# Layer 0's x and the later x 64 bytes apart in one array, a head's diagonal and first level in one matmul, and another order of layer 0

## The chip, the core and the metric

The kernel runs on one core of a Trainium2 chip, in one launch. The metric is the device time of that launch in microseconds (us). Before the change it is 2133.09 us, the median of three runs (2132.8 to 2133.53).

## What is computed

A decoder trunk of two layers in float32 for 256 tokens of 2048 features. Layer 0 has two kinds of mixer side by side, fed by one projection. The change touches the second kind, the HGRN2 heads (8 heads, 128 wide), and the order in which both kinds are worked off. Cut to these:

```python
def recurrent_mixers(h, w_in, ...):
    proj = h @ w_in
    x_lru, y_lru, q_h, f_h, v_h, g_h = jnp.split(proj, list(IN_SPLITS), axis=-1)
    lru = rg_lru(causal_depthwise_conv(x_lru, conv_w, conv_b), w_a, b_a, w_i, b_i, lam)
    lru = lru * jax.nn.gelu(y_lru, approximate=True)
    hg = hgrn2(q_h, f_h, v_h, g_h, lower_bound, g_norm)
    return jnp.concatenate([lru, hg], axis=-1) @ w_out

def hgrn2(q_raw, f_raw, v_raw, g_raw, lower_bound, g_norm):
    q = jax.nn.silu(q_raw)
    log_f = jnp.log(lower_bound + (1.0 - lower_bound) * jax.nn.sigmoid(f_raw))
    k = (1.0 - lower_bound) * jax.nn.sigmoid(-f_raw)
    ...  # scores[t, s] = sum over features of q[t] k[s] f[s+1]...f[t], for s <= t
    o = scores @ v
    o = o * rsqrt(mean(o * o) + NORM_EPS) * g_norm
    return o * jax.nn.silu(g_raw)
```

After the mixers come the output projection, a squared-ReLU MLP, a second layer with dilated attention and another MLP, and a last norm.

## The kernel before

**Matmuls.** The weights arrive as float32 in units of 128 x 2048. Each unit is split into a high part (`hi`, a cast on ScalarE, L112) and the rest (`lo`, a subtraction on VectorE, L113). The activations are split in the same way, and three matmuls, all by L196, stand for one product. x of layer 0 lies in `bufa`, 16 blocks of 2 x 256 columns. Later the same array holds the inputs of layer 0's MLP, of the attention and of layer 1's MLP. Where the output is wanted by features (`project`, L346), x is the moving operand with 256 columns; where it is wanted by tokens (`tokens_group`, L339), the weights move with 512.

**Layer 0.** `ORDER` (L1077) lists the steps: `v` and `k` are four units each for the values and gates of four heads, `h` is a head (two units, q and f), `x` and `y` are an LRU block's input and output (one unit each), `g` is the two LRU gates of four blocks, with one unit of small weights and `bufb` as the moving operand. The same list orders the weights' loads on SP's queue, two units ahead of their use. The order of single instructions on each engine is then made by a scheduler, which puts the matmuls of one head between those of the following projections.

**A head** (`hgrn`, L436). With q, k and f over the features (128 partitions) and 256 tokens, the scores are built by doubling. `pd` (L454) is the product of k and q of which the diagonal is kept (L456). Then for c = 1, 2, 4, ... 128 two matmuls of 64 columns (L470, and L465 with 128 columns for the last) give the scores between neighbouring blocks of c tokens. They are put into `st` under a mask (L473) or by copies (L478, L480), q and k are multiplied by the products of f over a block (L487), and those products are doubled (L489). Before level 1 q is multiplied by f (L458). At the end `po` multiplies the scores with the values (L494 to L496), and the result is normed and turned by TensorE (L508) into `bufb`. A matmul of f32 operands shows as two records of TensorE, each with a weight load; the projections' show as one.

Of the kernel before, what the change touches and what calls it, by code (L numbers as in the profile page):

```python
# [10 lines left out]
F32 = mybir.dt.float32  # L11
F32R = mybir.dt.float32r
# [4 lines left out]
OP = mybir.AluOpType  # L17
# [3 lines left out]
P = 128  # L21
S = 256
D = 2048
KB = D // P
# [18 lines left out]
def trunk_kernel(ctx, tc, begin, xtok, cols, tab, masks, pos, fin, w_in, w_gate, w_out, w_qkv, w_o, w1, w2, out):  # L43
# [3 lines left out]
    act = pool("act")  # L47
# [11 lines left out]

    xall = act.tile([P, KB * S], F32, name="xall")  # L60
    xres = xall.rearrange("p (j d) -> p j d", j=2)
    bufa = act.tile([P, KB, 2 * S], F32R, name="bufa")

    units = []
    made = {}
# [102 lines left out]
    def fetch_first():  # L168
        r = opening.tile([P, 14, WIDE], F32, name="first")
        e = wraw.tile([P, 2048], F32, name="raw")[:, :2 * WIDE].rearrange("p (k s) -> p k s", s=WIDE)  # L170
        homes = [r[:, k] for k in range(14)] + [e[:, k] for k in range(2)]
        nc.sync.dma_start(r[:, 0, :S], begin[:, 0, :S])
        nc.sync.dma_start(r[:, 0, S:], begin[:, 0, S:])
        for k in range(1, 4):
            nc.sync.dma_start(r[:, k], begin[:, k])
        for k in range(4, 16, 2):
            nc.sync.dma_start(r[:, k:k + 2] if k < 14 else e, begin[:, k:k + 2])
        for u in range(4):
            at[0] += 1
            w = made[u] = Weights(None, 0)  # L180
            for k in range(4 * u, 4 * u + 4):
                split_to(bufa[:, k], homes[k][:, :S], col("nmix0", k))
                w.split((k - 4 * u) * 512, 512, homes[k][:, S:])

    def unit(src, i):
# [52 lines left out]
    def split_to(dst, src, gain=None):  # L238
        if gain is None:
            h, l = dst[..., :S], dst[..., S:]  # L240
            A.copy(h, src)
            V.tensor_tensor(l, src, h.bitcast(F32), OP.subtract)
        else:
            A.activation(dst[:, :S], src, AF.Copy, scale=gain)
            V.scalar_tensor_tensor(dst[:, S:], src, gain, dst[:, :S].bitcast(F32),  # L245
                                   op0=OP.mult, op1=OP.subtract)
# [89 lines left out]
        return ps  # L336

    def tokens_group(src, i0, rt=None, by_k=False, name="vg"):
        ps = tokens(src, i0, bufa, by_k)  # L339
        v = vgs.tile([P, 2, 512], F32, name=name)  # L340
        with urgent():
            for j in range(2):
                A.activation(v[:, j], ps[j], AF.Copy, scale=1.0 if rt is None else rt[:, j:j + 1])
        return v

    def project(src, i, mov):  # L346
        w = unit(src, i)
        p = pmm.tile([P, 512], F32, name="p")
        direct(p, w, [(k, mov[:, k], k == 0, k == KB - 1) for k in range(KB)])
        return p  # L350
# [85 lines left out]
    def hgrn(hd, vg, gg):  # L436
        u0 = 20 + (hd // 4) * 16 + (hd % 4) * 2
        oml = omlb[:, hd:hd + 1]
        qk = wk.tile([P, 2 * S], F32, name="qk", bufs=3)
        qp, kq = qk[:, :S], qk[:, S:]  # L440
        p = project(w_in, u0, bufa)
        z = normed(p, "hz", 4)
        lut(qp, z, AF.Sigmoid)
        V.scalar_tensor_tensor(qp, z, oml, qp, op0=OP.mult, op1=OP.mult)
        p = project(w_in, u0 + 1, bufa)
        z = normed(p, "hz", 4)
        f = wk.tile([P, S], F32, name="f", bufs=3)
        lut(f, z, AF.Sigmoid)
        lut(kq, z, AF.Sigmoid, scale=-1.0)
        V.tensor_scalar(f, f, oml, lb[:, hd:hd + 1], op0=OP.mult, op1=OP.add)  # L450
        pd = psc.tile([P, 2, P], F32, name="pd", bufs=1)
        for j in range(2):
            js = slice(j * P, j * P + P)
            T.matmul(pd[:, j], kq[:, js], qp[:, js], start=True, stop=True)  # L454
        st = wk.tile([P, 3, P], F32, name="st", bufs=3)
        V.tensor_tensor(st[:, :2], pd, ident[:, None, :].to_broadcast([P, 2, P]), OP.mult)  # L456
        stf = st[:, :2].rearrange("p a b -> p (a b)")
        V.tensor_tensor(qp, qp, f, OP.mult)  # L458
        c = 1
        tot = f  # L460
        while c <= 128:
            pl = psc.tile([P, 2, 64], F32, name="pl", bufs=2)
            if c == 128:
                plf = pl.rearrange("p j c -> p (j c)")
                T.matmul(plf, kq[:, :P], qp[:, P:], start=True, stop=True)  # L465
                A.copy(st[:, 2], plf)
                break
            for j in range(2):
                js = slice(j * P, j * P + P)
                T.matmul(pl[:, j], kq[:, js], halves(qp[:, js], c, True), start=True, stop=True)  # L470
            if c <= 16:
                lv = LEVELS.index(c)
                V.copy_predicated(halves(stf, c, True), msk[:, lv].rearrange("p (n c) -> p n c", c=c),  # L473
                                  pl.rearrange("p j (n c) -> p (j n) c", c=c))
            elif c == 32:
                for n in range(2):
                    ps_ = slice(64 * n, 64 * n + 32)
                    A.copy(st[ps_, :2, 64 * n + 32:64 * n + 64], pl[ps_, :, 32 * n:32 * n + 32])  # L478
            else:
                A.copy(st[:64, :2, 64:], pl[:64])  # L480
            n = S // (2 * c)
            tt = tot.rearrange("p (n two) -> p n two", two=2)
            both = bass.AP(tensor=qk.tensor, offset=qk.offset + c,
                           ap=[list(qk.ap[0]), [S - c, 2], [2 * c, n], [1, c]])
            fac = bass.AP(tensor=tot.tensor, offset=tot.offset,
                          ap=[list(tot.ap[0]), [1, 2], [2, n], [0, c]])
            V.tensor_tensor(both, both, fac, OP.mult)  # L487
            nt = wk.tile([P, n], F32, name=f"tot{n}", bufs=2)
            V.tensor_tensor(nt, tt[:, :, 0], tt[:, :, 1], OP.mult)  # L489
            tot = nt  # L490
            c *= 2
        vs = slice((hd % 4) * P, (hd % 4) * P + P)
        po = psc.tile([P, 2, P], F32, name="po", bufs=1)
        T.matmul(po[:, 0], st[:, 0], vg[:, 0, vs], start=True, stop=True)  # L494
        T.matmul(po[:, 1], st[:, 2], vg[:, 0, vs], start=True, stop=False)  # L495
        T.matmul(po[:, 1], st[:, 1], vg[:, 1, vs], start=False, stop=True)  # L496
        o = wk.tile([P, 2, P], F32, name="ho", bufs=2)
        hs = wk.tile([P, 2], F32, name="hs", bufs=2)
        for j in range(2):
            A.activation(o[:, j], po[:, j], AF.Square, accum_out=hs[:, j:j + 1])  # L500
        V.tensor_scalar(hs, hs, 1.0 / P, EPS, op0=OP.mult, op1=OP.add)
        hr = wk.tile([P, 2], F32, name="hr", bufs=2)
        rsqrt(hr, hs, 2)
        for j in range(2):
            V.scalar_tensor_tensor(o[:, j], po[:, j], hr[:, j:j + 1], gg[:, j, vs], op0=OP.mult, op1=OP.mult)
        pt = psc.tile([P, 2, P], F32, name="pt", bufs=1)
        for j in range(2):
            T.transpose(pt[:, j], o[:, j], ident)  # L508
        split_to(bufb[:, 8 + hd], pt.rearrange("p j c -> p (j c)"), col("gn", hd))
# [1 line left out]
    xc = wk.tile([P, 8, S], F32, name="xc", bufs=1)  # L511

    def lru_in(b):
        p = project(w_in, b, bufa)
        xp = wk.tile([P, S + 4], F32, name="xp", bufs=1)
        V.memset(xp[:, :4], 0.0)
        scaled(p, xp[:, 4:])
        A.activation(xc[:, b], xp[:, 4:], AF.Identity, bias=col("conv_b", b), scale=col("conv_w", 24 + b))
        for i in range(3):
            V.scalar_tensor_tensor(xc[:, b], xp[:, 1 + i:1 + i + S], col("conv_w", 8 * i + b), xc[:, b],  # L520
                                   op0=OP.mult, op1=OP.add)
        split_to(bufb[:, b], xc[:, b])
# [24 lines left out]
            V.tensor_tensor_scan(xc[:, b], gr[:, m], xc[:, b], 0.0, op0=OP.mult, op1=OP.add)  # L547

    def lru_out(b):
        p = project(w_in, 8 + b, bufa)  # L550
        y = tmp.tile([P, S], F32, name="z")
        scaled(p, y)
        q = wk.tile([P, S], F32, name="q", bufs=1)
        A.activation(q, y, AF.Square, scale=math.sqrt(0.044715))
        V.scalar_tensor_tensor(q, q, 1.0, y, op0=OP.add, op1=OP.mult)
        lut(q, q, AF.Sigmoid, scale=2.0 * math.sqrt(2.0 / math.pi))
        V.tensor_tensor(y, y, q, OP.mult)
        V.tensor_tensor(y, y, xc[:, b], OP.mult)
        split_to(bufb[:, b], y)
# [509 lines left out]

LAST = 2  # L1070
EARLY = 12
BOUNDARY = 56
PRIO = 150
URGENT = 400
ATTENTION = "qqvqqv"
ORDER = "v0 k0 h0 h1 h2 x1 x3 h3 x0 k1 v1 x2 h4 x4 g0 x5 h5 h6 x6 y0 y1 h7 x7 g1 y3 y7 y4 y2 y5 y6"
WARM = 12  # L1077
WAIT_H, WAIT_X, WAIT_Q, WAIT_S = 5, 2, 5, 3
SCRATCH = 4096
# [109 lines left out]
```

## Time and profile before

| | us |
|---|---|
| median of three runs | 2133.09 |
| the profiled execution | 2133.06 |
| its span, first to last instruction | 2131.3 |
| TensorE busy in it | 2120.9 |
| VectorE busy | 1788.8 |
| ScalarE busy | 1378.2 |

Layer 0's mixers take about the first 332 us; the output projection begins there. A row of the timeline has a start in us from the start of the span, a length from the first start to the last end of its instructions, the engine, the line, what is written and read, the shape and a count. TensorE's instructions overlap, so two rows are compared by their starts. PEld is TensorE's weight load.

### The profile page before, as it was taken

Reading aid. Unit: us, or ns where it says so; the run is one execution under the profiler, and the core shown is the slowest. Engines: PE = TensorE matmul, PEld = TensorE weight load, DVE = VectorE, ACT = ScalarE, POOL = GpSimd, SP = SyncE. Lnnn points to the kernel's source line nnn. Section 1 sums busy time; section 2 is a strip of 40 time slices with the busy share of each in tenths; the row PEclk is TensorE's granted clock in tenths of the full one; section 3 lists DMA queues with packets and bytes.
Section 4 is the critical chain, followed back from the end, with each engine's and each line's share of the span. In section 5 each row is a group of like instructions: output and inputs, shape, how many; then the busy total and the mean of one; then the engine's idle time right before and its main releaser. Section 6 shows DMA issues by size and latency. Waiting matters only on the chain.

```text
span 2131.3 us, 26730 instructions
## 1 busy us (share of the span) xinstructions
PE 2120.9 (100%) x10542; PEld 1797.6 (84%) x10542; DVE 1788.8 (84%) x1962; ACT 1378.2 (65%) x1543; POOL 66.8 (3%) x85
## 2 busy tenths in 40 slices
PE   9999999999999999999999999999999999999998
PEld 8989998888888888888888888888888888888886
DVE  7777888888888888888988797788897888888887
ACT  7445565776476567567666777776756765755764
POOL 0000000000000000000000000000000000000000
PEclk9999999999999999999999999999999999999999
DMA  8444446686777677677887767777767768777773
GB/s 336 162 162 158 161 148 224 206 269 233 227 237 253 230 240 253 227 241 231 270 279 218 241 199 247 254 247 228 246 237 253 236 212 269 238 234 227 271 225 146
DMA packets 69806, 488.71 MB, mean 229 GB/s; under 512 B 7808, under 2 KB 8320, under 8 KB 11952
## 3 DMA queue, kind: packets, MB, share of 16 engines
q1 hardware_dynamic: 58176, 410.96, 51.1%
q0 software_dynamic: 11216, 75.70, 18.3%
q8 instruction: 82, 1.34, 0.3%
q14 instruction: 44, 0.36, 0.0%
q10 hardware_dynamic: 288, 0.34, 0.0%
HBM read 482.78 MB, written 4.19 MB: 228 GB/s over the span
## 4 chain that ended last, share of the span: by engine, by line
PE 99%; DVE 0%; ACT 0%; DMA 0%; issue 0%; ACTq 0%; DVEq 0%; POOLq 0%
PE p L196 62%; PE po L196 14%; PE pd L196 13%; PE pt L196 5%; PE pl L199 2%; PE pl L470 1%; PE pl L196 0%; PE pd L199 0%; DMA ppi<-in_pos 0%; PE pd L454 0%; DVE lo L113 0%; ACT hi L112 0%; PE pl L465 0%; PE po L495 0%; PE po L496 0%
## 5 line engine op out<-in xcount | busy, mean ns | idle before, releaser
L113 DVE TENSOR_TENSOR lo<-raw,hi 128x2048 fp32r<-128x2048 f32 (+2 forms) x397 | 787.1, 1991 | 164.5 <-ACT hi L112 159.4
L112 ACT CAST hi<-raw 128x2048 fp32r<-128x2048 f32 (+2 forms) x397 | 657.3, 1671 | 335.1 <-PE p L196 175.5
L196 PE MATMUL p<-hi,bufa 128*128 128x512 f32 x1488 | 482.0, 394 | 0.0
L196 PE MATMUL p<-hi,bufb 128*128 128x512 f32 x1128 | 363.1, 391 | 0.0
L196 PEld LDWEIGHTS p<-hi,bufa 128*128 128x128 f32 x1488 | 279.2, 188 | 57.3 <-DVE bufa L245 0.5
L113 DVE TENSOR_TENSOR lo<-s,hi 128x2048 fp32r<-128x2048 f32 (+1 forms) x164 | 285.9, 1753 | 28.6 <-ACT hi L112 27.6
L112 ACT CAST hi<-s 128x2048 fp32r<-128x2048 f32 (+1 forms) x164 | 242.7, 1480 | 98.2 <-DVE s L164 54.2
L196 PE MATMUL p<-lo,bufa 128*128 128x512 f32 x744 | 287.6, 390 | 0.2 <-DVE lo L113 0.2
L196 PEld LDWEIGHTS p<-hi,bufb 128*128 128x128 f32 x1128 | 211.7, 188 | 43.7
L196 PE MATMUL p<-lo,bufb 128*128 128x512 f32 x564 | 219.5, 389 | 0.0
L196 PE MATMUL p<-bufa,hi 128*128 128x256 f32 x1024 | 193.2, 287 | 0.0
L196 PEld LDWEIGHTS p<-lo,bufa 128*128 128x128 f32 x744 | 139.9, 188 | 28.0 <-DVE lo L113 0.7
L196 PEld LDWEIGHTS p<-bufa,hi 128*128 128x128 f32 x1024 | 161.2, 191 | 0.2
L196 PE MATMUL p<-bufa,lo 128*128 128x256 f32 x512 | 146.5, 286 | 0.0
L112 ACT CAST hi<-t 128x2048 fp32r<-128x2048 f32 x41 | 78.5, 1914 | 99.6 <-PE p L196 91.1
L113 DVE TENSOR_TENSOR lo<-t,hi 128x2048 fp32r<-128x2048 f32 x41 | 94.0, 2292 | 55.4 <-ACT hi L112 55.0
L196 PEld LDWEIGHTS p<-lo,bufb 128*128 128x128 f32 x564 | 105.9, 188 | 21.5
L196 PE MATMUL p<-hi,formh 128*128 128x512 f32 x368 | 120.7, 391 | 0.0
L196 PE MATMUL p<-hi,formx 128*128 128x512 f32 x352 | 115.9, 390 | 0.0
L196 PE MATMUL po<-hi,bufb 128*128 128x512 f32 x320 | 103.7, 390 | 0.0
L196 PEld LDWEIGHTS p<-bufa,lo 128*128 128x128 f32 x512 | 98.0, 191 | 0.0
L164 DVE TENSOR_TENSOR s<-s,raw 128x1024 f32<-128x1024 f32 x82 | 96.4, 1216 | 0.1
(319 smaller groups left out, 3292.4 us busy)
## 6 DMA issues: line engine op xcount, KB each, us to landing
raw<-in_w SPq DMA_DIRECT2D x224, 1024.0 KB, 6.1
raw<-in_w_in SPq DMA_DIRECT2D x44, 1024.0 KB, 4.8
raw<-in_w_qkv SPq DMA_DIRECT2D x42, 1024.0 KB, 6.9
t<-in_w SPq DMA_DIRECT2D x32, 1024.0 KB, 4.9
t<-in_w POOLq DMA_DIRECT2D x32, 1024.0 KB, 8.7
s<-in_w POOLq DMA_DIRECT2D x17, 1024.0 KB, 8.4
raw<-in_w_out SPq DMA_DIRECT2D x15, 1024.0 KB, 4.8
raw<-in_w_o SPq DMA_DIRECT2D x14, 1024.0 KB, 7.7
```

The source lines that it names most:

```text
L112: a = A.copy(h, w)
L113: v = V.tensor_tensor(l, w, h.bitcast(F32), OP.subtract)
L164: V.tensor_tensor(s, s, held["c"][:, at:at + 1024], OP.add)
L196: chain[:] = [after(T.matmul(*args, **kw), chain)]
L199: chain[:] = [after(T.transpose(out_, in_, ident), chain)]
L470: T.matmul(pl[:, j], kq[:, js], halves(qp[:, js], c, True), start=True, stop=True)
```

## The change

Three edits. First, the array for x is 16 floats (64 bytes) longer. Layer 0 reads and writes it from its start (`bufx`), everything later 64 bytes further on (`bufa`). What is allocated behind it moves by 64 bytes. Second, a head keeps q in groups of three: the two tokens of a pair, and the second one multiplied by its f. One matmul of 192 columns for each half of the tokens then gives the diagonal and level 1 together, and the loop of levels starts at c = 2. Third, `ORDER` is another one.

```diff
-    bufa = act.tile([P, KB, 2 * S], F32R, name="bufa")
+    bufa_ = act.tile([P, KB * 2 * S + APART], F32R, name="bufa")
+    bufx, bufa = (bufa_[:, o:o + KB * 2 * S].rearrange("p (k c) -> p k c", k=KB) for o in (0, APART))
...
-        V.scalar_tensor_tensor(qp, z, oml, qp, op0=OP.mult, op1=OP.mult)
-        p = project(w_in, u0 + 1, bufa)
+        q3 = wk.tile([P, P, 3], F32, name="q3", bufs=2)
+        pairs_ = lambda t: t.rearrange("p (n two) -> p n two", two=2)
+        V.scalar_tensor_tensor(q3[:, :, :2], pairs_(z), oml, pairs_(qp), op0=OP.mult, op1=OP.mult)
+        p = project(w_in, u0 + 1, bufx)
...
-        pd = psc.tile([P, 2, P], F32, name="pd", bufs=1)
+        f2 = pairs_(f)
+        V.tensor_tensor(q3[:, :, 2], q3[:, :, 1], f2[:, :, 1], OP.mult)
+        pd = psc.tile([P, P, 3], F32, name="pd", bufs=1)
         for j in range(2):
-            js = slice(j * P, j * P + P)
-            T.matmul(pd[:, j], kq[:, js], qp[:, js], start=True, stop=True)
+            js = slice(64 * j, 64 * j + 64)
+            T.matmul(pd[:, js].rearrange("p n c -> p (n c)"), kq[:, j * P:j * P + P],
+                     q3[:, js].rearrange("p n c -> p (n c)"), start=True, stop=True)
         st = wk.tile([P, 3, P], F32, name="st", bufs=3)
-        V.tensor_tensor(st[:, :2], pd, ident[:, None, :].to_broadcast([P, 2, P]), OP.mult)
+        V.tensor_tensor(st[:, :2].rearrange("p j (n two) -> p j n two", two=2),
+                        pd[:, :, :2].rearrange("p (j n) c -> p j n c", j=2),
+                        pairs_(ident)[:, None].to_broadcast([P, 2, 64, 2]), OP.mult)
         stf = st[:, :2].rearrange("p a b -> p (a b)")
-        V.tensor_tensor(qp, qp, f, OP.mult)
-        c = 1
-        tot = f
+        V.copy_predicated(halves(stf, 1, True), msk[:, 0].rearrange("p (n c) -> p n c", c=1), pd[:, :, 2:])
+        V.tensor_tensor(pairs_(qp), q3[:, :, ::2], f2[:, :, :1].to_broadcast([P, P, 2]), OP.mult)
+        V.tensor_tensor(pairs_(kq)[:, :, 0], pairs_(kq)[:, :, 0], f2[:, :, 1], OP.mult)
+        tot = wk.tile([P, P], F32, name="tot128", bufs=2)
+        V.tensor_tensor(tot, f2[:, :, 0], f2[:, :, 1], OP.mult)
+        c = 2
...
+APART = 16
...
-ORDER = "v0 k0 h0 h1 h2 x1 x3 h3 x0 k1 v1 x2 h4 x4 g0 x5 h5 h6 x6 y0 y1 h7 x7 g1 y3 y7 y4 y2 y5 y6"
+ORDER = "v0 k0 h0 h1 h2 x1 x3 x2 h3 x0 v1 k1 h4 h5 h6 x4 g0 x5 x6 y0 h7 y1 x7 y2 g1 y7 y4 y3 y5 y6"
```

The other changed lines put `bufx` for `bufa` in layer 0's projections. In the new program lines are numbered a little higher (L196 becomes L197, L470 becomes L481, L494 to L496 become L505 to L507). The lists below are parts of the instruction order of the two built programs; x2 is a count. From the output projection on, TensorE's list is the same in both.

TensorE at the second head's diagonal, before (`pd` the diagonal, `pl` a level, `p` a projection):

```order
L196 MATMUL p<-bufa,lo 128x256
L196 MATMUL p<-bufa,hi 128x256
L454 MATMUL pd<-qk 128x128
L470 MATMUL pl<-qk 128x64 x2
L454 MATMUL pd<-qk 128x128
L196 MATMUL p<-bufa,hi 128x256
```

The same place now:

```order
L197 MATMUL p<-bufa,lo 128x256
L197 MATMUL p<-bufa,hi 128x256
L481 MATMUL pl<-qk 128x64 x2
L459 MATMUL pd<-q_825,qk 128x192 x2
L197 MATMUL p<-bufa,hi 128x256
```

The diagonal's two matmuls have 192 columns, and a head has six levels of two 64-column matmuls where it had seven.

TensorE at group 1 of the LRU gates (moving operand `bufb`), before. `po` is the end of head 6, the `pl` of 128x128 its last level, and the `pl` of 128x64 levels of head 7:

```order
L196 MATMUL p<-bufb,hi 128x256 x2
L196 MATMUL p<-bufb,lo 128x256
L494 MATMUL po<-vg,st 128x128
L465 MATMUL pl<-qk 128x128
L470 MATMUL pl<-qk 128x64 x2
L495 MATMUL po<-vg,st 128x128
L496 MATMUL po<-vg,st 128x128
L196 MATMUL p<-bufb,hi 128x256
L470 MATMUL pl<-qk 128x64 x2
L196 MATMUL p<-bufb,hi 128x256
```

The first rows of group 1 now. Between this pair of level matmuls and the next there are 15 gate matmuls, then 24 to the one after:

```order
L197 MATMUL p<-bufb,hi 128x256 x2
L197 MATMUL p<-bufb,lo 128x256
L481 MATMUL pl<-qk 128x64 x2
L197 MATMUL p<-bufb,hi 128x256 x2
L197 MATMUL p<-bufb,lo 128x256
```

Only levels of head 7 stand between the gates of group 1 now; the last level and the end of a head have moved out of them.

TensorE at group 0 of the gates, before (the end of head 3 and a level of head 4):

```order
L196 MATMUL p<-bufb,lo 128x256
L465 MATMUL pl<-qk 128x128
L494 MATMUL po<-vg,st 128x128
L470 MATMUL pl<-qk 128x64 x2
L196 MATMUL p<-bufb,hi 128x256 x2
```

And now (`pd` is the diagonal of head 6, `po` and the `pl` of 128x128 the end of head 5):

```order
L197 MATMUL p<-bufb,hi 128x256 x2
L459 MATMUL pd<-q_2421,qk 128x192 x2
L197 MATMUL p<-bufb,lo 128x256
L197 MATMUL p<-bufb,hi 128x256 x2
L197 MATMUL p<-bufb,lo 128x256
L197 MATMUL p<-bufb,hi 128x256
L505 MATMUL po<-vg,st 128x128
L197 MATMUL p<-bufb,hi 128x256
L476 MATMUL pl<-qk 128x128
L481 MATMUL pl<-qk 128x64 x2
```

A head's diagonal has come in among the gates of group 0, close to the end of another head.

More of the change, by code (lines that the diff above doesn't have):

```diff
@@ L181, in fetch_first @@
             for k in range(4 * u, 4 * u + 4):
-                split_to(bufa[:, k], homes[k][:, :S], col("nmix0", k))
+                split_to(bufx[:, k], homes[k][:, :S], col("nmix0", k))
                 w.split((k - 4 * u) * 512, 512, homes[k][:, S:])
@@ L338, in tokens_group @@
     def tokens_group(src, i0, rt=None, by_k=False, name="vg"):
-        ps = tokens(src, i0, bufa, by_k)
+        ps = tokens(src, i0, bufx, by_k)
         v = vgs.tile([P, 2, 512], F32, name=name)
@@ L440, in hgrn @@
         qp, kq = qk[:, :S], qk[:, S:]
-        p = project(w_in, u0, bufa)
+        p = project(w_in, u0, bufx)
         z = normed(p, "hz", 4)
         lut(qp, z, AF.Sigmoid)
-        V.scalar_tensor_tensor(qp, z, oml, qp, op0=OP.mult, op1=OP.mult)
-        p = project(w_in, u0 + 1, bufa)
+        q3 = wk.tile([P, P, 3], F32, name="q3", bufs=2)
+        pairs_ = lambda t: t.rearrange("p (n two) -> p n two", two=2)
+        V.scalar_tensor_tensor(q3[:, :, :2], pairs_(z), oml, pairs_(qp), op0=OP.mult, op1=OP.mult)
+        p = project(w_in, u0 + 1, bufx)
         z = normed(p, "hz", 4)
@@ L513, in lru_in @@
     def lru_in(b):
-        p = project(w_in, b, bufa)
+        p = project(w_in, b, bufx)
         xp = wk.tile([P, S + 4], F32, name="xp", bufs=1)
@@ L549, in lru_out @@
     def lru_out(b):
-        p = project(w_in, 8 + b, bufa)
+        p = project(w_in, 8 + b, bufx)
         y = tmp.tile([P, S], F32, name="z")
```

## The prediction

> **What bounds the kernel now.** I read the page's busy times first, then its chain of work, then a table of stages (the windows view: busy time and instruction count of each engine in a stretch).
>
> ```profile
> PE 2120.9 (100%) x10542; PEld 1797.6 (84%) x10542; DVE 1788.8 (84%) x1962; ACT 1378.2 (65%) x1543; POOL 66.8 (3%) x85
> PE 99%; DVE 0%; ACT 0%; DMA 0%; issue 0%; ACTq 0%; DVEq 0%; POOLq 0%
> 51.40:100.00 48.60, 48.60 (x410) 48.60 (x409) 34.89 (x72) 21.45 (x33) 0.00 (x0) 1.00 0.48 172
> 200.00:250.00 50.00, 50.00 (x426) 50.00 (x425) 44.98 (x124) 34.07 (x65) 0.00 (x0) 1.00 0.43 149
> 282.00:289.00 7.00, 6.74 (x52) 6.05 (x51) 6.41 (x16) 5.64 (x16) 0.00 (x0) 1.00 0.42 149
> 332.00:2131.00 1799.00, 1790.43 (x8155) 1485.14 (x8153) 1531.90 (x1321) 1188.13 (x1198) 65.89 (x80) 1.00 0.73 237
> ```
>
> TensorE is busy all the time and is 99% of the chain, at the full clock. VectorE comes next, with free time in every stage (45 of 50 us at most). A time is won here only if TensorE issues less, or if a wait between its matmuls goes. Nothing behind about 332 us can change by the edits: in the lists of the built programs TensorE's rows from the output projection to the end are the same ones in the same order, so those 1799 us stay. What follows is about the first 332 us, the mixers of layer 0.
>
> TensorE's busy time hides small waits, because the ends of pipelined matmuls are modelled. I therefore count from start to start. First the prices of one matmul. From the chain in order of time (start, us, what), two runs of 512 columns, the first with bufa's tiles and the second with bufb's:
>
> ```profile
> 447.79 5.44 PE pd L196 x24
> 552.07 13.60 PE p L196 x60
> ```
>
> TensorE's timeline (start, us from first start to last end, count) around a level of a head and around a diagonal; each x2 that "..." leaves out is two hi of 256 columns:
>
> ```profile
> 71.15 0.28 PE L196 MATMUL p<-bufa,lo 128*128 128x256 f32 x1
> ...
> 71.51 0.28 PE L196 MATMUL p<-bufa,lo 128*128 128x256 f32 x1
> ...
> 71.87 0.55 PE L470 MATMUL pl<-qk 128*128 128x64 f32 x4
> 72.23 0.36 PE L196 MATMUL p<-bufa,lo 128*128 128x256 f32 x1
> ...
> 72.68 0.28 PE L196 MATMUL p<-bufa,lo 128*128 128x256 f32 x1
> ...
> 67.83 0.28 PE L196 MATMUL p<-bufa,lo 128*128 128x256 f32 x1
> 67.95 0.28 PE L196 MATMUL p<-bufa,hi 128*128 128x256 f32 x1
> 68.07 0.61 PE L454 MATMUL pd<-qk 128*128 128x128 f32 x4
> 68.43 0.36 PE L196 MATMUL p<-bufa,hi 128*128 128x256 f32 x1
> 68.63 0.28 PE L196 MATMUL p<-bufa,lo 128*128 128x256 f32 x1
> ```
>
> 512 columns take 13.60 / 60 = 0.227 us, and 5.44 / 24 as well. 256 columns take 0.12 (71.15 to 71.51 is one lo and two hi). One f32 matmul of a head shows as two records, so x4 is two matmuls. From the lo at 71.15 to that at 72.68 are 1.53 us, of which nine matmuls of 256 columns are 1.08, so four records of 64 columns cost 0.45. From 67.83 to 68.63 are 0.80 us, three of them 256-column ones (0.36), so four records of 128 columns cost 0.44. Both are **0.11 us a record**: below 128 columns a head's matmul costs the same whatever its width.
>
> **Part 1: one matmul of 192 columns in place of 128 and 64.** Each of 8 heads loses four records of level 1 (0.44) and has its diagonal's four records widened from 128 to 192. No row has 192. The nearest on the wide side are the attention scores of layer 1, where x4 is two records of 128 and two of 256:
>
> ```profile
> 1154.29 0.39 PE L196 MATMUL p<-lo,bufa 128*128 128x512 f32 x1
> 1154.51 0.39 PE L196 MATMUL p<-hi,bufa 128*128 128x512 f32 x1
> 1154.74 0.81 PE L196 MATMUL pl<-kT,qT 128*128 128x128 f32 x4
> 1155.21 0.58 PE L196 MATMUL pt<-hi,formx 128*128 128x512 f32 x1
> 1155.62 0.39 PE L196 MATMUL pt<-lo,formx 128*128 128x512 f32 x1
> ```
>
> 1155.62 - 1154.29 = 1.33 us, less three matmuls of 512 columns (0.68), less two records of 128 (0.22), leaves 0.43 or 0.215 a record of 256. So 192 lies between 0.11 and 0.215. I take the middle, 0.163, since 128 and 256 are equally near. A head then pays 4 x 0.163 = 0.65 where it paid 0.44 + 0.44 = 0.88: 0.23 less, **1.8 us in eight heads**. With 0.11 it would be 3.5, with 0.215 only 0.2.
>
> [...]
>
> **VectorE in a head.** The rows of before for what is replaced (durations least/median/most, in ns):
>
> ```profile
> L487 DVE TENSOR_TENSOR qk<-qk,tot x48: 396/418/474, 77.9 to 312.6; 128x256 f32<-128x256 f32 x48
> L487 DVE TENSOR_TENSOR qk<-qk,f x8: 451/462/473, 73.2 to 287.9; 128x256 f32<-128x256 f32 x8
> L489 DVE TENSOR_TENSOR tot<-f x8: 278/284/291, 66.8 to 279.0; 128x128 f32<-128x128 f32 x8
> L458 DVE TENSOR_TENSOR qk<-qk,f x8: 412/414/416, 69.1 to 281.3; 128x256 f32<-128x256 f32 x8
> L473 DVE COPY_PREDICATED st<-msk,pl x40: 273/301/449, 73.0 to 302.8; 128x128 f32<-128x128 int8 x40
> ```
>
> The multiply by f (0.414) and level 1's multiply on every second element (0.462) go. One multiply of 256 elements (0.414 to 0.462) and two of 128 (0.284) come. The other operations stay and now step by three. A step of two cost 0.462 against 0.418, so I add 0.05 to each of five: about +0.36 us a head, 2.9 in eight. The other end is the slowest predicated copy, 0.449 against a median of 0.301, half as much again, about 1 us a head. In the stage's fullest stretch VectorE has 5 us of 50 free, so I cost this at nothing. The diagonal's matmul now also waits for one multiply of 128 elements more (0.28), while level 2 no longer waits for a result of level 1. Behind the waiting diagonal stand the next unit's projection matmuls; that wait has the same cover as the diagonal has now, so nothing again, with 0.28 a head (2.3) if the cover were gone.
>
> **Part 2: the order of the units.** At group 1 of the gates the old order puts five insertions of two heads side by side, in the shortest matmul sequences of the stage:
>
> ```profile
> 282.94 0.28 PE L196 MATMUL p<-bufb,lo 128*128 128x256 f32 x1
> ...
> 286.07 0.38 PE L494 MATMUL po<-vg,st 128*128 128x128 f32 x2
> 286.64 0.49 PE L465 MATMUL pl<-qk 128*128 128x128 f32 x2 [0.19 <-DVE qk L487]
> 286.97 0.56 PE L470 MATMUL pl<-qk 128*128 128x64 f32 x4
> 287.49 0.49 PE L495 MATMUL po<-vg,st 128*128 128x128 f32 x2
> ...
> 289.05 0.28 PE L196 MATMUL p<-bufb,lo 128*128 128x256 f32 x1
> ```
>
> Who waited for whom between 282 and 289 (us in total, times, longest):
>
> ```profile
> PEld pl L465 <- DVE qk L487: 0.4, 1, 0.4
> ...
> PEld pl L470 <- DVE qk L487: 0.3, 1, 0.3
> ...
> PEld p L196 <- ACT bufb L241: 0.2, 1, 0.2
> ```
>
> Between the two lo at 282.94 and 289.05 lie 6.11 us. They hold 18 matmuls of 256 columns (2.16) and 24 records of heads (2.64), together 4.80: **1.3 us are waits**, and the rows of waits in this stretch name a head's multiply (L487) and a cast. In the new order the same place (the lists in the section on the change) has one pair of level matmuls with 15, then 24 gate matmuls between them, and no end of another head. I take the 1.3 us as gone. What is late next is group 0, where an end of one head and a diagonal of the next now meet. The old order also has a head's end there, and the rows of waits of the whole stage name none at that place, so 0 is my value, 1.3 the bound. One more wait stands at 309.77 in the timeline:
>
> ```profile
> 309.37 0.28 PE L196 MATMUL p<-bufa,lo 128*128 128x256 f32 x1
> ...
> 309.77 0.66 PE L470 MATMUL pl<-qk 128*128 128x64 f32 x4
> 310.24 0.37 PE L196 MATMUL p<-bufa,lo 128*128 128x256 f32 x1
> ```
>
> From lo to lo it is 0.87 here, and 0.72 in the undisturbed case (71.51 to 72.23): 0.15 more, under the last head, which is also spread wider now. The weights' loads move with their units on SP's queue, 14 rows of it in all. The DMA engines are 0.42 to 0.48 busy in this stage (last column but one of the stages), so I cost that at nothing.
>
> **Part 3: 64 bytes.** Every tile behind x moves by 64 bytes, and in layer 0 x stands 64 bytes nearer to its start against all of them; later it does not. 256 columns more cost 0.227 - 0.120 = 0.107 us, so 0.120 holds 0.013 that is no column. This fixed part is the same with bufa as with bufb (both runs above). No row has a shift of 64 bytes, so the bounds are that it goes or doubles in layer 0's 2,028 such matmuls (counted in the built program): 27 us either way. I take 0, the value of every row that there is.
>
> **Sum.** 1.8 + 1.3 + 0.15 = 3.25 us less. The profiled execution took 2133.06 us (span 2131.3 and 1.8 around it), 0.03 from the median. Forecast: **2129.8 us**.
>
> **Rivals.**
> - Waits come back. At group 0, or where gates now follow y2, a head's multiply is late again: 1.3 us, as at 282 to 289. For: the added step-by-three operations. Against: three heads in a row (51 to 100 us) leave VectorE 14 of 49 us free. Time 2131.1. [...]
> - Columns are the price. If the 192 columns cost as 256 do, only the waits and 0.2 go: 2131.4.
> - The shift slows layer 0. Weights and x are read side by side; if their new distance makes them meet, the fixed 0.013 us grows. At +1.6 ns a matmul the gain is eaten, at +3.7 ns the kernel is slower by over 0.2%, and at half of the bound, 13.5 us, it takes **2143 us**. For: the fixed part is a whole 32 columns' time, which looks like a meeting of two reads. Against: it is equal for all tiles.
> - The shift speeds layer 0, by the same argument: 2116 at half.
>
> [...]
>
> **How the numbers follow.** Forecast 0.63, waits back 0.13, columns 0.06, shift slower 0.07, shift faster 0.11. The unknown price of 192 moves the forecast from 2128.1 to 2131.4, new waits to 2132.7, and a shift by 1 ns a matmul by 2 us either way. So 2126.0 to 2133.3, which leaves out most of both shift cases and 0.03 of the rest. 0.2% is 4.3 us, about what a measurement can tell from no change. Faster by more: the quick shift and a tenth from 192's cheap end, 0.21. Slower by more: 0.07. Between: 0.72.
>
> **What would show it.** A diagonal's x4 inserted for 0.65 us, lo to lo; no start-to-start excess at the gates of group 1 or 0; 256 columns still at 0.12; VectorE's step-by-three operations at 0.45 to 0.52. A run of 256 columns at another spacing, or a wait on a head's multiply, would make it wrong.

## The result, and the profile after

| | before | changed |
|---|---|---|
| median of the runs, us | 2132.77 (6 runs, 2132.25 to 2133.53) | 2125.08 (6 runs, 2124.87 to 2125.81) |
| ratio, 95% interval | | 0.9965 (0.9955 to 0.9975) |
| the profiled execution, us | 2133.06 | 2125.05 |
| its span, us | 2131.3 | 2123.2 |
| first matmul of the output projection, us | 329.3 | 321.2 |

The change saves 7.7 us, 0.36%. The forecast was 3.25 us less, with a range down to 2126.0: the sign was right, the size was not, and the time lies just outside. The page of the changed kernel, its busy times:

```profile
PE 2112.4 (99%) x10510; PEld 1788.9 (84%) x10510; DVE 1788.8 (84%) x1970; ACT 1377.4 (65%) x1543; POOL 66.7 (3%) x85
```

TensorE still sets the time: it is busy for 99% of the span and makes up 97% of the page's chain. Its stages in the windows view (stretch, length, busy time and count of PE, PEld, DVE, ACT, POOL, clock, share of the DMA engines, GB/s):

```profile
51.22:100.00 48.78, 48.78 (x423) 48.77 (x422) 38.01 (x82) 21.90 (x37) 0.00 (x0) 1.00 0.52 176
200.00:250.00 50.00, 49.72 (x427) 49.52 (x426) 42.61 (x110) 30.38 (x58) 0.00 (x0) 1.00 0.43 148
282.00:289.00 7.00, 7.00 (x62) 7.00 (x61) 6.58 (x22) 5.42 (x14) 0.00 (x0) 1.00 0.40 147
321.00:2123.00 1802.00, 1793.39 (x8168) 1487.51 (x8166) 1535.73 (x1328) 1190.48 (x1202) 65.85 (x80) 1.00 0.74 237
```

The first stretch holds 423 matmuls in 48.78 us where it held 410 in 48.60, at the same clock (1.00), and the rows of waits name none of TensorE's in it. That is the surprise, and a run of 256-column matmuls in the chain, before any head comes between, shows it (start, us, what):

```profile
52.99 13.03 PE p L197 x115
```

13.03 / 115 = 0.1133 us a matmul, where the prediction had 0.12 throughout. The places that the prediction named, from TensorE's timeline: the second head's diagonal, then group 1 of the gates.

```profile
68.47 0.28 PE L197 MATMUL p<-bufa,lo 128*128 128x256 f32 x1
68.58 0.28 PE L197 MATMUL p<-bufa,hi 128*128 128x256 f32 x1
68.69 0.81 PE L459 MATMUL pd<-q,qk 128*128 128x192 f32 x4
69.21 0.42 PE L197 MATMUL p<-bufa,hi 128*128 128x256 f32 x1
69.46 0.28 PE L197 MATMUL p<-bufa,lo 128*128 128x256 f32 x1
...
284.18 0.28 PE L197 MATMUL p<-bufb,lo 128*128 128x256 f32 x1
284.30 0.55 PE L481 MATMUL pl<-qk 128*128 128x64 f32 x4
...
286.54 0.55 PE L481 MATMUL pl<-qk 128*128 128x64 f32 x4
...
289.74 0.28 PE L197 MATMUL p<-bufb,lo 128*128 128x256 f32 x1
```

From lo to lo at the diagonal are 0.99 us; less three matmuls at 0.1133 this leaves 0.65 for four records of 192 columns, the forecast's figure. From 284.18 to 289.74 are 5.56 us, and 39 matmuls of 256 columns (4.68) with eight records of 64 (0.88) are 5.56 too: the waits at group 1 are gone. Over bufb 256 columns still take 0.12 (0.1194 on the mean of 79 uninterrupted steps, 0.1196 before); only those over x became shorter.

### The profile page after: what moved, and what is told of

Read it like the earlier page. It is cut to its first block, busy times and chain, and to the rows that moved or that the text cites. A ratio compares the mean times of both kernels' runs of the same rounds, so it can differ in the third digit from the quotient of the medians.

```text
span 2123.2 us, 26672 instructions
## 1 busy us (share of the span) xinstructions
PE 2112.4 (99%) x10510; PEld 1788.9 (84%) x10510; DVE 1788.8 (84%) x1970; ACT 1377.4 (65%) x1543; POOL 66.7 (3%) x85
## 4 chain that ended last, share of the span: by engine, by line
PE 97%; ACT 1%; DVE 1%; DMA 0%; issue 0%; SPq 0%; ACTq 0%; DVEq 0%
PE p L197 61%; PE po L197 14%; PE pd L197 13%; PE pt L197 5%; PE pl L200 2%; PE pl L481 1%; PE pl L197 0%; ACT hi L113 0%; DMA first<-in_begin 0%; ACT gi L226 0%; PE pd L459 0%; PE pd L200 0%; ACT L226 0%; ACT gr L226 0%; DVE xc L558 0%
## 5 line engine op out<-in xcount | busy, mean ns | idle before, releaser
L197 PE MATMUL p<-hi,bufa 128*128 128x512 f32 x1488 | 481.8, 394 | 0.2 <-ACT hi L113 0.2
L197 PE MATMUL p<-hi,bufb 128*128 128x512 f32 x1128 | 362.9, 391 | 0.0
L197 PEld LDWEIGHTS p<-hi,bufa 128*128 128x128 f32 x1488 | 279.1, 188 | 58.0 <-ACT hi L113 0.6
L197 PE MATMUL p<-lo,bufa 128*128 128x512 f32 x744 | 288.6, 391 | 0.2 <-DVE lo L114 0.2
L197 PEld LDWEIGHTS p<-hi,bufb 128*128 128x128 f32 x1128 | 211.8, 188 | 43.7
L197 PE MATMUL p<-lo,bufb 128*128 128x512 f32 x564 | 219.5, 389 | 0.0
L197 PE MATMUL p<-bufa,hi 128*128 128x256 f32 x1024 | 186.6, 282 | 0.0
L197 PEld LDWEIGHTS p<-lo,bufa 128*128 128x128 f32 x744 | 139.9, 188 | 28.0 <-DVE lo L114 0.7
L197 PEld LDWEIGHTS p<-bufa,hi 128*128 128x128 f32 x1024 | 157.9, 189 | 0.2
L197 PE MATMUL p<-bufa,lo 128*128 128x256 f32 x512 | 144.4, 282 | 0.0
L197 PEld LDWEIGHTS p<-lo,bufb 128*128 128x128 f32 x564 | 105.9, 188 | 21.4
L197 PE MATMUL p<-hi,formh 128*128 128x512 f32 x368 | 120.7, 391 | 0.0
L197 PE MATMUL p<-hi,formx 128*128 128x512 f32 x352 | 116.0, 391 | 0.0
L197 PE MATMUL po<-hi,bufb 128*128 128x512 f32 x320 | 103.8, 390 | 0.0
L197 PEld LDWEIGHTS p<-bufa,lo 128*128 128x128 f32 x512 | 96.5, 188 | 0.0
```

Source lines behind the costliest of these rows:

```text
L197: chain[:] = [after(T.matmul(*args, **kw), chain)]
```

## The experiments

Every difference is to the kernel before, run beside it. "In the run" is the mean from start to start inside uninterrupted runs of layer 0, counted from the traces: f, 256 columns over x (some 1,400 each); t, 512 columns over x in the first 51 us (some 180).

| run | what it has | median, us | to before, us | ratio, 95% interval | f, ns | t, ns |
|---|---|---|---|---|---|---|
| before | | 2132.77 | | | 119.8 | 226.8 |
| apart_only | array | 2128.95 | -3.57 | 0.9974 to 0.9992 | 116.3 | 232.5 |
| order_only | order | 2136.75 | +4.23 | 1.0012 to 1.0030 | 119.8 | 227.0 |
| heads_only | heads | 2132.48 | -0.21 | 0.9988 to 1.0006 | 119.8 | 226.8 |
| no_apart | heads, order | 2128.97 | -3.55 | 0.9974 to 0.9992 | 119.8 | 226.7 |
| no_order | array, heads | 2127.71 | -4.98 | 0.9968 to 0.9986 | 115.6 | 229.0 |
| apart_32 | all, 32 bytes | 2128.62 | -4.22 | 0.9972 to 0.9990 | 118.3 | 233.3 |
| apart_88 | all, 88 bytes | 2147.47 | +14.93 | 1.0059 to 1.0083 | 118.3 | 233.4 |
| changed | all | 2125.08 | -7.69 | 0.9955 to 0.9975 | 115.6 | 229.0 |
| after_again | all | 2125.11 | -7.43 | 0.9953 to 0.9977 | 115.2 | 229.0 |

### The array alone, and the change without it

apart_only is the kernel before with the first edit of the diff and nothing else. no_apart is the changed kernel with

```diff
-APART = 16
+APART = 0
```

> The kernel before with the first edit alone: x's array 64 bytes longer, layer 0 at its lower end. Theory A (the distance between x and the weights in SBUF sets the fixed part of a 256-column matmul): the spacing of layer 0's 256-column matmuls over x falls from 120 ns to 113 to 118 as in the changed kernel, those over bufb stay at 120, the 512-column ones of layer 0 rise by 2 to 3 ns; by the sums of the changed kernel's trace (5.4 us less, 0.9 more) the time is 4.5 us lower, 2128.3 (4.0 to 5.0 lower). The waits at group 1 of the gates, 1.3 us, stay. Theory B (the new heads and the new order take load off SBUF, and that is why the matmuls come closer): 120 ns and no change, 2132.8.

> The changed kernel with the array not lengthened (the second and third edit alone). Theory A: the spacing of the 256-column matmuls goes back to 120 ns, and what is left is the forecast of the prediction without the shift: 1.8 to 2.0 us from the heads and 1.3 to 1.5 us from the waits, 3.1 to 3.5 us less than before, 2129.5. Theory B: the spacing stays at 113 to 118 and the time at 2125.

The same stretch of the chain as above, in apart_only:

```profile
52.90 13.19 PE p L197 x112
```

and in no_apart:

```profile
52.99 13.08 PE p L197 x109
```

0.1178 and 0.12 us a matmul. The shorter spacing comes with the array and goes with it, and neither heads nor order touch it: theory B is out. The array is worth 3.57 us alone (4.5 were expected, 4.0 at the least), 4.14 on top of the rest (7.69 - 3.55) and 4.77 on top of the heads (4.98 - 0.21). Heads and order together are worth 3.55, the prediction's sum without the shift within 0.3.

Part of what apart_only lacks is in the 512 columns. The first run of them over x, in apart_only and then in the changed kernel:

```profile
8.60 34.10 PE p L197 x145
8.30 33.46 PE p L197 x145
```

That is 0.64 us at the same distance. From start to start apart_only has 233.3 ns through 143 steps here and 229.1 in its next run, from 43 us on; the changed kernel has 229 in both. So at this distance 512 columns have been seen at two spacings, and the distance alone does not say which one comes.

### The order alone

```diff
-ORDER = "v0 k0 h0 h1 h2 x1 x3 h3 x0 k1 v1 x2 h4 x4 g0 x5 h5 h6 x6 y0 y1 h7 x7 g1 y3 y7 y4 y2 y5 y6"
+ORDER = "v0 k0 h0 h1 h2 x1 x3 x2 h3 x0 v1 k1 h4 h5 h6 x4 g0 x5 x6 y0 h7 y1 x7 y2 g1 y7 y4 y3 y5 y6"
```

> The kernel before with the new order of layer 0 alone, heads and array as they were. Theory A: the waits at group 1 of the gates and the one at 309.8 us go, 1.3 to 1.5 us, and no new wait of over 0.3 us comes: 2131.4. Rival (the new order puts a wait elsewhere, at group 0 of the gates for one): no gain or under 0.5 us, 2132.5, with an excess from start to start at that place. In both, 256 columns at 120 ns.

Both missed: it is 4.23 us slower. The output projection begins at 327.5, 1.8 us earlier than before (1.3 to 1.5 were forecast), and 7.5 us later it stands still. TensorE's waits between 325 and 350 us (in all, times, longest):

```profile
PE p L196 <- DVE bufb L245: 2.0, 1, 2.0
PE p L196 <- ACT bufb L244: 1.6, 1, 1.6
```

L244 and L245 put the last head's turned result into `bufb`. The timeline there:

```profile
331.39 0.60 DVE L505 SCALAR_TENSOR_TENSOR ho<-po,hr,gg 128x128 f32<-128x128 f32 x2
335.06 0.38 PE L508 MATMUL pt<-tab__199,ho 128*128 128x128 f32 x2
337.05 0.50 PE L196 MATMUL p<-hi,bufb 128*128 128x512 f32 x1 [1.62 <-ACT bufb L244]
339.23 0.48 DVE L245 SCALAR_TENSOR_TENSOR bufb<-pt,c__82,bufb 128x256 fp32r<-128x256 f32 x1
339.76 0.73 PE L196 MATMUL p<-hi,bufb 128*128 128x512 f32 x2 [1.97 <-DVE bufb L245]
```

The norm of head 7 (`ho`) ends at 332 us. In the built program the two turns of head 7 (L508) stand behind 33 matmuls of the projection, which are over the seven other heads' blocks of `bufb`; the matmul over head 7's block comes right behind them, and those over the LRU's eight blocks come later. The turns start at 335.06, 3 us behind the norm, when the list has come to them, and TensorE then stands still until the turned result is in `bufb`; its subtraction, on VectorE behind a weight's split and three other operations, starts at 339.23. In the kernel before the turns stand behind 9 and 11 matmuls of the projection, in no_apart and in the changed kernel ahead of it. So the lists from the output projection on, called the same ahead of the prediction and in it, differ in these two rows, and the wait hangs on just them.

When TensorE goes on, it is slow for a while. A stretch of order_only in the windows view:

```profile
341.00:344.50 3.50, 3.50 (x10) 2.69 (x9) 2.96 (x8) 1.14 (x2) 0.00 (x0) 0.52 0.34 133
```

The granted clock (the column behind POOL) is 0.52, where the kernel before has 1.00 from 336 to 345 us, and ten matmuls take 3.5 us. Matmul by matmul against the kernel before, the projection loses 2.0 us at the first wait, 2.1 at the second and 1.6 in this stretch, 5.8 in all. It began 1.8 earlier, so the profiled execution is 4.0 us longer.

In the built programs head 7's last `po` stands behind 1,962 of the 2,016 projection matmuls ahead of the output projection in the order alone, behind 1,913 in the kernel before, 1,877 in no_apart and 1,827 in heads_only. With the new heads it comes 85 matmuls earlier in the new order and 86 in the old one, so the earlier end is the heads' doing. That it is the missing level of their chain which does it was not tried by itself.

### The heads alone, and the change without its order

heads_only is the changed kernel with both lines, no_order with the second:

```diff
-APART = 16
+APART = 0
-ORDER = "v0 k0 h0 h1 h2 x1 x3 x2 h3 x0 v1 k1 h4 h5 h6 x4 g0 x5 x6 y0 h7 y1 x7 y2 g1 y7 y4 y3 y5 y6"
+ORDER = "v0 k0 h0 h1 h2 x1 x3 h3 x0 k1 v1 x2 h4 x4 g0 x5 h5 h6 x6 y0 y1 h7 x7 g1 y3 y7 y4 y2 y5 y6"
```

> The kernel before with the new heads alone (order as before, array not lengthened). The order alone cost 4.2 us, by waits of the output projection for the last head's turned result, which in its instruction lists stands 85 projection matmuls later than in the kernel with both. Theory C (each edit has a price of its own and they add up): heads alone are 3.5 + 4.2 = 7.8 us faster, 2124.8. Theory D (the heads are worth the matmuls that they save, 2.0 us by the changed kernel's trace, and what they did beside that was to bring the last head's end forward, which the new order needs and the old one doesn't): waits at group 1 of the gates as before, 1.3 us, no wait at the output projection, 2130.5; at the most 2131.5 if the heads' ends meet more closely in group 1.

> The changed kernel with the old order (new heads and longer array). Theory D: as heads_only, with the shift's 3.6 to 3.9 us less (two runs so far), 2126.6 to 2127.9: slower than the changed kernel by 1.5 to 2.8 us, the waits at group 1 of the gates there again. Theory C: 2121, faster than the changed kernel.

Prices do not add up: by the medians the heads gain 0.2 us alone (theory C wanted 7.8, theory D 1.2 to 2.2) and 7.8 in the new order (4.23 + 3.55). heads_only at group 1 of the gates, where "..." leaves out four records of `po` and one hi:

```profile
285.16 0.28 PE L197 MATMUL p<-bufb,lo 128*128 128x256 f32 x1
...
286.23 0.66 PE L481 MATMUL pl<-qk 128*128 128x64 f32 x4 [0.35 <-DVE qk L498]
287.73 0.39 PE L197 MATMUL p<-bufb,hi 128*128 128x256 f32 x1 [0.84 <-ACT bufb L242]
287.99 0.63 PE L481 MATMUL pl<-qk 128*128 128x64 f32 x4
...
288.63 0.28 PE L197 MATMUL p<-bufb,lo 128*128 128x256 f32 x1
```

From lo to lo are 3.47 us, three matmuls of 256 columns and twelve records are 1.68, so 1.8 us are waits where the kernel before had 1.3. With the old order the heads' saving is partly eaten there. The runs of heads_only differ by their granted clock: five at 0.999 took 2130.98 to 2131.48 us, six at 0.998 took 2132.48 to 2133.29. The five, of which the trace is one, are 1.2 to 1.7 us below the kernel before, as theory D had it. An estimate: 3.5 us at a clock of 0.52, as order_only has them, would cost 1.7 us (3.5 x 0.48), about what the six lose, and lower the mean clock by 0.001 (1.7 / 2131); no trace of one of them is there, so this is likely and not shown. The median of no_order lies in theory D's bounds; its runs spread from 2126.46 to 2129.57.

### Matmuls alone at other distances

offsets and offsets_fine leave the trunk out; each ran once. One tile serves as weights, one as x; both are read at an offset of some bytes, and nothing else runs:

```python
def features(p, m, s):      # f: 256 columns of x moving
    for k in range(16):
        for j, (a, b) in enumerate(((0, 0), (0, 256), (2048, 0))):
            x = xt[:, m + k * 512 + b:m + k * 512 + b + 256]
            h = wt[:, s + a + k * P:s + a + k * P + P]
            mm(p[:, :256], h, x, start=not k and not j, stop=k == 15 and j == 2)
```

> A kernel of its own that leaves the trunk out: only matmuls over two tiles, one as weights and one as x, in the pattern of layer 0 (f rows: 256 columns of x moving, 128 of the weights loaded; t rows: 512 columns of the weights moving, 128 of x loaded), 96 for each pair of byte offsets (x's, the weights'), on an otherwise idle core. Theory A1 (only the distance between the two counts): f0_0, f64_64, f32_32 and the other f0_0 all at 120 ns, f0_64, f448_0 and f32_96 alike at 113 to 118. Theory A2 (the position of x or of the weights by itself counts, not their distance): f64_64 differs from f0_0, or f0_64 from f32_96. Theory A3 (the spacing depends on what the other engines read and write at the same time): all f rows alike. The offsets between give the period. For the t rows the changed kernel's trace has 229 in place of 226.7 ns at 64 bytes; an offset with less than 226.7 ns would be worth 13 ns in each of some 7,500 matmuls at the most.

> Matmuls only, the trunk is left out: x below the weights by 8 to 96 bytes in steps of 8 (all that there is room for in the kernel) and by 128, 144, 160, above them by 8, 24, 40, 56 and 112, and level with them; each in eight stretches of 19 to 48 matmuls behind different interruptions by f32 matmuls. Of 64 bytes below the first sweep showed 113.3 or 117.8 ns, by the stretch. Theory E (which of the two comes is set by the moment at which the weight load and the moving operand start after an interruption): at 64 both are seen among the eight stretches, always one of the two through a stretch; the level case is 120 in all eight. Theory F (chance or other traffic): the spacing varies inside a stretch, or between equal stretches. A distance below 96 with 113.3 in all eight stretches, and t rows not above 228.9, would be worth up to 1,470 x 2.4 = 3.5 us more in the kernel. 112 above (= 144 below if the period is 256) gave 113.3 in both stretches of the first sweep: E with period 256 has the two rows alike.

Chain of offsets, f rows, two stretches each at the offsets (x, weights) of (64, 64), (0, 64), (32, 32) and (32, 96):

```profile
209.03 5.81 PE f L37 x48
...
215.23 5.81 PE f L37 x48
...
221.43 5.71 PE f L37 x48
...
227.53 5.71 PE f L37 x48
...
233.63 5.80 PE f L37 x48
...
239.83 5.80 PE f L37 x48
...
246.01 5.51 PE f L37 x48
...
251.91 5.51 PE f L37 x48
```

At (64, 64) and (32, 32) the time is that of (0, 0), and no other engine is needed (A3 is out). At 64 bytes below, (0, 64) has 5.71 and (32, 96) 5.51, which was named as a sign of A2, by which the place counts. But both times also come at one place, here the two stretches at the offsets (448, 0), which is 64 below modulo 256:

```profile
197.03 5.50 PE f L37 x48
...
202.93 5.71 PE f L37 x48
```

So the place is not needed to explain the two times; for multiples of 32 the distance (A1) explains the rest. The t rows, the first with x 64 bytes above, the second level at (32, 32):

```profile
421.24 11.25 PE t L37 x48
...
697.67 10.97 PE t L37 x48
```

Means from start to start of both sweeps, in ns:

```
x above the weights by (bytes)    f                t
   0                            120.0            226.8
 -64                            113.3 or 117.8   228.9
 -32, -96                       118.2, 118.0     233.4, 233.3
  -8                            115.6            233.2
 +64                            117.8            233.3
  +4                            123.4            232.4
+112                            114.5            233.2
-144                            119.9            233.3
```

0 and 256 are alike (f 120.0), 64 and 320 (117.8), 192 and 448 (113.3 or 117.8), so for these the period is 256 bytes. But +112 and -144, which differ by 256 and are no multiples of 32, are not alike for f (114.5 and 119.9); what decides there stays open. For 512 columns level is the best of all that were tried (226.8), and x below by 64 the next (228.9). At -64 the fine sweep has both times in stretches behind different interruptions, and each holds to its end; here 25, then 24 matmuls:

```profile
238.79 2.85 PE fbelow L38 x25
...
242.03 2.88 PE fbelow L38 x24
```

### What picks the one or the other

gaps is the same kernel at 64 bytes below throughout, with ten kinds of interruption, and ran once.

> Matmuls only (the trunk is left out), x 64 bytes below the weights throughout. Before each of 16 stretches of 18 to 31 matmuls of 256 columns stands one kind of interruption by f32 matmuls, ten kinds of it: one of 64 columns, one of 128, two of 64 (a level of a head), 64 and 128, 128 and 64, two of 128, two of 96, two of 16, four of 64, two of 192 (the new diagonal). Theory E (the moment at which the stream is taken up again picks 113.3 or 117.8 ns, until the next interruption): each stretch shows one of the two, and the share of the slow one goes with the kind; in the changed kernel 15 of 25 stretches behind a level were slow, and none of two behind a diagonal alone. Theory G (it is set by chance): all ten kinds have about the same share. A kind with no slow stretch at the same cost would be worth up to 650 x 4.5 = 2.9 us in the kernel.

Behind a single f32 matmul of 128 columns (24, 25, 26 matmuls):

```profile
85.38 2.83 PE single L38 x24
...
88.44 2.85 PE single L38 x25
...
91.51 3.06 PE single L38 x26
```

0.118, 0.114, 0.118: the two times alternate, stretch by stretch, in 16 stretches. So they do behind one of 64 and behind two of 96 or of 192 columns. Behind two of 16, 64 or 128, behind 64 and 128 in either order, and behind four of 64, all 16 stretches are at 117.8. Inside this program the kind counts, against theory G, and each time holds until the next interruption (E).

From program to program the kind does not decide. In offsets two matmuls of 64 stand before every stretch, and of the eight at 64 below four are at 113.4 and four at 117.8. In offsets_fine the three stretches at that distance behind 64 and 128 are all at about 113.5. Even one program can have either: the changed kernel and after_again are the same, and up to 304 us their stretches have the same spacings, but not in the last long run over x:

```profile
304.80 14.96 PE p L197 x127
304.94 14.42 PE p L197 x127
```

0.1178 in the changed kernel, 0.1135 in after_again. So something beyond the kind of the interruption has a part in it, which no run here shows. In the changed kernel 695 of the 1,413 uninterrupted steps of f are 113 or 114 ns long, about half. No kind was always quick, so nothing cheaper to put between offers itself.

### Two other distances in the kernel

```diff
-APART = 16
+APART = 8        (apart_32; 22 in apart_88)
```

> The changed kernel with 32 bytes between layer 0's x and the later one in place of 64. If the sweeps of matmuls alone carry over: 256 columns at 118.2 ns (115.7 on the mean in the changed kernel) and 512 columns of layer 0 at 233.4 (229 to 231 there), so 1,470 x 2.5 + 370 x 3.5 = 3.7 + 1.3 = 5.0 us slower than the changed kernel: 2130.1, no better than the kernel without any shift (2129.0). If only the fact of a shift counts and not its size: 2125.1.

> The changed kernel with 88 bytes between layer 0's x and the later one in place of 64, the one other distance under 96 at which the fine sweep came as low: 256 columns at 114.8 ns there (115.6 on the mean in the changed kernel), 512 columns at 231.8 (228.9). If these carry over: 1,470 x 0.8 = 1.2 us less, 190 x 2.9 + 175 x 2.2 = 0.9 us more, 0.3 us faster than the changed kernel, 2124.8, which is hardly to be told from it. If 32 bytes' miss (3.5 us slower than the changed kernel, where 5.0 were expected) repeats, within 1.5 us of that.

> The changed kernel once more, beside the kernel before on the same chip and in the same call as the 88 bytes: 7.5 to 7.9 us under the kernel before.

apart_32 has the sweep's f and t (118.3, 233.3) and is 3.5 us slower than the changed kernel, not 5.0: the size of the distance counts. apart_88 did not try what it was meant to. In the built program the tiles behind x lie 96 bytes further on, not 88 (the first `hi` at byte 80,768, without the shift at 80,672), so layer 0's x is 96 below the weights and the later x 8 below. It tries the sweeps' values at two distances for that. In its chain, 24 matmuls of 512 columns over the later x, and 24 over another tile, whose distance has not changed:

```profile
444.37 5.60 PE pd L197 x24
...
571.61 5.44 PE po L197 x24
```

0.2333 and 0.2267 us, as the t rows say for -8 and 0. All 2,841 recorded intervals of that sort take 670.2 us where the changed kernel has 654.0. These 16.2 are most of the 22.4 us to after_again; another 3.9 are the 256-column intervals of layer 0. What fits for layer 0 and leaves the later x level are 32, 64 and 96 bytes; 64 is the best of them by the sweeps (96 with a level later x was not run in the kernel), and no version faster than the changed kernel came out. after_again is 7.43 us under the kernel before, a little short of the 7.5 to 7.9 expected.

## Why the prediction was wrong

**Part 1, the heads, 1.8 us: right in price.** The four records cost 0.65 as forecast. From start to start, `pd` and the 64-column `pl` take 21.73 us in no_apart and 23.86 in the kernel before, 2.1 less. VectorE's new operations, in the changed kernel (least/median/most, ns):

```profile
L455 DVE TENSOR_TENSOR q<-q,f x8: 317/330/336, 66.0 to 268.6; 128x128 f32<-128x128 f32 x8
L466 DVE COPY_PREDICATED st<-msk,pd x8: 433/438/441, 72.0 to 274.6; 128x128 f32<-128x128 int8 x8
L467 DVE TENSOR_TENSOR qk<-q,f x8: 414/416/419, 66.5 to 269.1; 128x256 f32<-128x256 f32 x8
```

The step of three costs less than was put on it. The copy's 0.438 is what level 1's copy took before (0.435 to 0.448; the median of 0.301 in the prediction mixes five levels), and the 0.416 of L467 is that of the multiply that it replaces. Only L455 is dearer, 0.330 where another multiply of this size (L468) takes 0.282. All of it stays hidden: the profile of the changed kernel names nobody that waited for L455, L466 or L467. What the prediction did not see is that the new heads move the last head's end forward, on which the order depends.

**Part 2, the order, 1.3 + 0.15 us: right in the sum, wrong as a price of its own.** The waits at group 1 are gone in the changed kernel, and group 0 stayed clear: the one wait left between 200 and 300 us is 0.3 us at 248.7, for a head's multiply under projections. But with the old heads the same order costs 4.2 us, at a place that the prediction called unchangeable ("Nothing behind about 332 us can change by the edits"). Two rows of TensorE's list do move there, the turns of head 7, and what the others wait for comes from the heads. With both edits the wait does not arise, so the sentence nearly held for the changed kernel by the heads' help. That the sum of the two parts came out is in this respect luck.

**Part 3, 64 bytes, 0 us: the step that failed.** "I take 0, the value of every row that there is" read 0.013 us of fixed part, equal with bufa and with bufb, as a sign that the place of a tile does not matter. In the built program x lies at byte 23,328, the first `hi` at 80,672 and bufb at 132,384: both distances are multiples of 256, so these rows had been taken at one and the same distance modulo 256 and could not speak of another. The rival "the shift speeds layer 0" (chance 0.11) was right, with a third of its 13.5 us. Between no_apart and the changed kernel, the 256-column intervals over x sum to 181.27 and 175.43 us, 5.8 less (4.0 ns in each); the steps from them to heads' matmuls take 0.65 more, the 512-column ones in layer 0 0.7 more. That leaves 4.5 us less, and the output projection begins 4.7 earlier; behind its start the changed kernel takes 0.5 longer than no_apart, for which no run shows the reason. The prediction counted 2,028 matmuls for this bound. The built program has 2,016, of which 1,536 have 256 columns over x, and only these gain. The sweeps of matmuls alone, from 113.3 to 123.4 ns for 256 columns where only offsets change, show the effect without the trunk. Weight loads and matmuls do run at the same time (PEld 48.77 and PE 48.78 busy in the 48.78 us of the first stretch above); whether the effect comes from the reads of the two meeting, as the prediction's rival had it, no run shows.

The sum of the first two parts, 3.25, stands beside 3.55 measured; the third was 0 and measured 4.1.

## What to carry to other kernels

A price that is the same in every row shows that nothing varied, not that nothing matters: look up what the rows have in common (here the distance of two tiles modulo 256 bytes) before a change of just that is put at zero. Two edits to one schedule are to be priced together, since the one may only pay where the other has moved the last wait. A list that is called the same should be compared to the last row: two moved rows decided here. Where matmuls fill the time, count them from start to start; busy time showed neither the shorter spacing (48.60 of 48.60 us before, 48.78 of 48.78 now) nor, at group 1, more than 0.26 of the 1.3 us of waits (6.74 of 7.00).

## What the runs showed of the hardware

With fp32r operands, the spacing of matmuls went with the distance between the weights loaded and the operand moving: in the sweeps, on an otherwise idle core, 113.3 to 123.4 ns for 256 columns and 226.8 to 233.4 for 512 at the distances in the table. At the multiples of 32 bytes that were tried 256 bytes apart it was the same (f 120.0 at 0 and 256, 117.8 at 64 and 320, 113.3 or 117.8 at 192 and 448). The best distance for the one width was not the best for the other: 256 columns had 113.3 at 64 bytes below and 120.0 level, 512 columns 228.9 and 226.8. At 64 bytes below 256 columns showed two steady spacings, 113.3 and 117.8 ns, and changed from one to the other only at an interruption by f32 matmuls, in the 16 stretches of each of ten kinds in gaps; 512 columns were seen at 229 and 233.3 there in the full kernel. What picks one of them, and what in the chip makes the distance count, no run here shows. In order_only two waits of TensorE, 1.6 and 2.0 us within some 5 us, were followed by 3.5 us at a granted clock of 0.52.
